# A two-layer hybrid decoder step: the second layer's heads with no arithmetic on GpSimd, rotary steps and weight splits one at a time, latents normalised once, and an opening in halves

## The chip, the core and the metric

The kernel runs on one core of one Trainium2 chip. The metric is the time of one execution on the device in microseconds. The engines are called by their names in the profile: PE is TensorE (matrix products and transposes), PEld its weight loads, DVE is VectorE, ACT is ScalarE, POOL is GpSimd, SP is SyncE, which here only issues transfers.

## What is computed

One inference step of a decoder with two layers of width 1024, for a prompt of 512 tokens and eight sample streams of four tokens each. Prompt and samples use the same weights, so the kernel keeps them as 512 + 32 = 544 columns. Cut to what matters here:

```python
# layer 0 (mixer A): input projection, pooling branch, memory attention, gates, output projection
# between the layers: one shared compressed key/value side
kv = rmsnorm(x, g_kv_in) @ w_kv_down
ckv, krope = rmsnorm(kv[..., :256], g_kv_latent), rope(kv[..., 256:])       # ranks 256 and 64
# layer 1 (mixer B): latent attention with 8 heads, and 4 heads into 256 memory tokens
z = rmsnorm(x, g_norm[1]) @ w_in_b
c_q, gate_t, q_m, gate_m = split(z)                                         # c_q has rank 384
q = (rmsnorm(c_q, g_q) @ w_q_up).reshape(T, 8, 128 + 64)
q_rope = rope(q[..., 128:])
q_lat = einsum('thd,chd->thc', q[..., :128], w_k_up)
s = (q_lat @ ckv.T + q_rope @ krope.T) * 192 ** -0.5                         # causal mask
o_lat = softmax(s) @ ckv
tok = einsum('thc,chd->thd', o_lat, w_v_up)
mixed = concatenate([tok * silu(gate_t), mem_o * silu(gate_m)])
x = x + mixed @ w_out[1]                                                    # then the last rmsnorm
```

The samples also attend, in layer 1, to 4096 earlier tokens each, which lie in a paged cache of 128 tokens a page (latent and rotary part, 32 pages to a stream).

## The kernel before

The stream is held with its features on the partitions. Products of 32-bit floats are made as three products of a reduced format: `split` (its lines are 89 and 90) writes a rounded copy, the high part, on ScalarE, and then the remainder, the low part, on VectorE or, where it is given that engine, on GpSimd. `mm3` (lines 94, 95 and 96) multiplies high by high, high by low, and low by high.

Up to the middle of the second layer a scheduler sets the order of the instructions on each engine. `normed` (lines 180 to 199) makes the two parts of the stream times the gain, one group of 128 features at a time, with `Copy` on ScalarE (line 198) and the remainder on VectorE (line 199). In the opening, `first_w` splits the first two units of weights between these steps, half a unit at a time; a unit (128x1024) is loaded whole, and line 177 (180 for later groups) is the square for the norm.

From the second layer's late gates to the output, the order on TensorE and on the queue of SP is written by hand: generators hand out pieces of TensorE's work, and `weave` picks at each step, among those that may go on, the one that is furthest behind its share. It keeps an estimated time `now` and estimated queues `act` and `dve` for ScalarE and VectorE, and a piece is taken only when its inputs are ready by these estimates. The generators are

- `round_scores` and `round_values`: sixteen rounds in which 16 pages of one stream are read from the cache (tiles `a` and `b`), some keys turned and copied (`kt`, line 1073 on ScalarE and 1076 on VectorE), the scores made (`ac`, line 1109), their maximum taken on VectorE (line 1118), the exponentials on ScalarE (`rt`, line 1120), turned again (TensorE line 135, copied by line 1135) and multiplied by the values (line 1143);
- `gates_late`: the last four gates of the layer, with `gate_part` (lines 264 and 265 are its sigmoid and its product);
- `head_inputs`: for each of the four pairs of heads a rotary projection (`q_proj`, whose eviction at line 1292 multiplies by the scale and the norm), the rotary step (`rope_T`: copies that swap halves at lines 767 and 768, products and the sum, here on GpSimd; then `qr`, a high part at line 1310 and a remainder on GpSimd at line 1311), and for each head its query and its key, and for each pair its values (`values`); every weight comes through `ahead`, is split with its remainder on GpSimd, and its successor's transfer is issued by GpSimd at that point (line 1212 for `qw`, line 1222 for `wu`);
- `scores` and `heads`: a head's own 512 by 512 scores (`hs`), softmax and output;
- `out_all`, `out_rows` and the rest: the output projection in twelve slabs of weights of 256 by 512, prepared by `prepare` three ahead, with the inputs split by `mix_b`.

Order and estimates are fixed when the kernel is built; on the chip each engine goes through its own list and waits where an input is late. The gates that the heads read late are stored to memory by GpSimd (`gd`, line 1202) and read back (`gl`, line 1375).

## Time and profile before

| what | value |
|---|---|
| time, three runs | 831.43, 831.79 and 832.11 us, median 831.79 |
| the profiled execution's own time | 830.44 us |
| its span, first to last instruction | 828.7 us |
| mean granted clock of TensorE | 0.985 of full speed |
| PE busy | 782.6 us, 94% of the span |
| DVE, ACT, POOL busy | 491.5, 316.1 and 236.2 us |
| moved by DMA | 169.54 MB, mean 205 GB/s |

The span in 40 equal slices (20.7 us each) gives the stages; each digit is the busy share in tenths, PEclk the granted clock in tenths of full speed:

```profile
PE   6999999999999999889999997899979989899995
...
DVE  6757667698834435866666644457675666742413
ACT  7453334432433325434333222345443445431212
POOL 0035221111234313303323244424232241024421
PEclk9999999999999999999999999899999999999997
```

The first layer takes the slices up to about 16, the shared key/value side and the second layer's projections run to about 480 us, the heads from about 490 to 722 us, and the output projection from there to the end. The chain of work that ended last, followed back from the last instruction, divides over the engines so:

```profile
PE 80%; DVE 9%; DMA 3%; ACT 3%; issue 2%; POOL 1%; SPq 1%; POOLq 0%; DVEq 0%; ACTq 0%
```

In the rows of the profile that list single instructions, the columns are start (us from the span's start), length, engine, line of the source, operation, output and inputs, shapes, how many of them, and in square brackets the idle time of the engine just before with what ended it. In rows that list groups, busy time and mean length in ns stand behind the bar.

### The profile page before, as it was taken

The page shows a single profiled execution, that of the slowest core. Times are in us where ns is not written, and L with a number is a line of the kernel's source. Part 1 is how long each engine was busy: PE and PEld are TensorE (multiplying, and loading weights), DVE is VectorE, ACT ScalarE, POOL GpSimd, SP SyncE. Part 2 cuts the span into 40 slices and gives each one's busy share as a digit, 9 for nine tenths or more (in the row PEclk, how much of TensorE's full clock was granted, in tenths as well). Part 3 has the DMA queues.
Part 4 walks back from the last instruction along what each step waited for, and adds up shares of the span by engine and source line. Part 5 has one row for each costly group of instructions (what it writes and reads, how often), then busy time and mean ns, then how long its engine had stood idle before and what let it go on. Part 6 is the DMA issues. An engine that isn't in the chain of part 4 may idle for free.

```text
span 828.7 us, 17366 instructions
## 1 busy us (share of the span) xinstructions
PE 782.6 (94%) x6814; PEld 666.3 (80%) x6814; DVE 491.5 (59%) x945; ACT 316.1 (38%) x631; POOL 236.2 (28%) x216
## 2 busy tenths in 40 slices
PE   6999999999999999889999997899979989899995
PEld 6989998999999989768998885567757766577774
DVE  6757667698834435866666644457675666742413
ACT  7453334432433325434333222345443445431212
POOL 0035221111234313303323244424232241024421
PEclk9999999999999999999999999899999999999997
DMA  8356247521232327436525799889868869893935
GB/s 308 95 181 226 77 178 256 159 80 63 78 96 79 100 97 230 142 127 204 204 77 206 241 352 368 297 275 334 294 228 300 302 219 353 299 343 106 327 111 177
DMA packets 82964, 169.54 MB, mean 205 GB/s; under 512 B 9409, under 2 KB 26434, under 8 KB 82626
## 3 DMA queue, kind: packets, MB, share of 16 engines
q1 hardware_dynamic: 76642, 148.04, 53.0%
q0 software_dynamic: 6240, 20.39, 6.7%
q8 instruction: 54, 0.88, 0.4%
q14 instruction: 28, 0.23, 0.1%
HBM read 157.19 MB, written 11.21 MB: 203 GB/s over the span
## 4 chain that ended last, share of the span: by engine, by line
PE 80%; DVE 9%; DMA 3%; ACT 3%; issue 2%; POOL 1%; SPq 1%; POOLq 0%; DVEq 0%; ACTq 0%
PE pa L94 16%; PE pa L96 16%; PE pa L95 15%; PE tr L135 4%; PE ac L1143 4%; PE ac L1109 3%; PE hs L94 2%; PE hs L96 2%; PE hs L95 2%; PE ac L1099 2%; PE ac L393 1%; DMA wr<-in_w_mem_v 1%; PE hs L135 1%; PE po L94 1%; DMA b<-in_cache_P 1%
## 5 line engine op out<-in xcount | busy, mean ns | idle before, releaser
L94 PE MATMUL pa<-h,wh 128*128 128x272 f32 x832 | 239.3, 290 | 0.0
L96 PE MATMUL pa<-h,wl 128*128 128x272 f32 x832 | 236.4, 289 | 1.2 <-POOL wl L90 1.2
L95 PE MATMUL pa<-h,wh 128*128 128x272 f32 x640 | 183.8, 288 | 0.0
L90 POOL TENSOR_TENSOR wl<-wr,wh 128x1024 fp32r<-128x1024 f32 (+1 forms) x54 | 121.9, 2257 | 188.9 <-ACT wh L89 185.8
L94 PEld LDWEIGHTS pa<-h,wh 128*128 128x128 f32 x832 | 156.4, 188 | 5.3 <-issue 4.3
L96 PEld LDWEIGHTS pa<-h,wl 128*128 128x128 f32 x832 | 155.0, 188 | 2.7 <-POOL wl L90 1.8
L89 ACT CAST wh<-wr 128x1024 fp32r<-128x1024 f32 (+1 forms) x87 | 87.7, 1008 | 180.5 <-PE pa L95 68.5
L95 PEld LDWEIGHTS pa<-h,wh 128*128 128x128 f32 x640 | 120.3, 188 | 0.9
L95 PE MATMUL pa<-g,wh 128*128 128x272 f32 x192 | 54.6, 289 | 0.7 <-DVE g L90 0.7
L90 DVE TENSOR_TENSOR wl<-wr,wh 128x1024 fp32r<-128x1024 f32 x33 | 40.4, 1223 | 16.4 <-ACT wh L89 16.3
L265 DVE SCALAR_TENSOR_TENSOR g<-t,g 128x272 f32<-128x272 f32 x40 | 36.0, 908 | 7.1 <-ACT t L264 7.1
L1143 PE MATMUL ac<-a,rt 128*32 128x256 f32 x384 | 37.1, 423 | 3.2 <-DVE rt L1135 3.2
L264 ACT ACTIVATE t<-g 128x272 f32<-128x272 f32 x40 | 16.6, 427 | 57.5 <-DVE g L251 57.5
L95 PEld LDWEIGHTS pa<-g,wh 128*128 128x128 f32 x192 | 36.2, 189 | 1.0 <-DVE g L90 1.0
L1143 PE MATMUL ac<-b,rt 128*32 128x256 f32 x128 | 36.8, 423 | 0.0
L1109 PE MATMUL ac<-kt,c 128*32 128x256 f32 x128 | 32.9, 380 | 2.6 <-ACT kt L1073 1.7
L1109 PE MATMUL ac<-a,c 128*32 128x256 f32 x384 | 33.4, 380 | 0.0
L1143 PEld LDWEIGHTS ac<-a,rt 128*32 128x32 f32 x384 | 14.3, 118 | 18.7 <-issue 6.9
L251 DVE SCALAR_TENSOR_TENSOR g<-pa,r 128x272 f32<-128x272 f32 x38 | 16.3, 437 | 21.6 <-PE pa L96 21.5
L1357 ACT ACTIVATE e<-hs,s 128x128 f32<-128x128 f32 (+3 forms) x32 | 16.9, 529 | 29.5 <-DVE s L1355 29.5
L95 PE MATMUL pa<-wl,mh 128*128 128x512 f32 x64 | 25.2, 402 | 1.0 <-DVE wl L90 1.0
L199 DVE SCALAR_TENSOR_TENSOR h<-x,c,h 128x544 fp32r<-128x544 f32 x24 | 19.6, 828 | 9.2 <-ACT h L198 9.1
(438 smaller groups left out, 1840.2 us busy)
## 6 DMA issues: line engine op xcount, KB each, us to landing
a<-in_cache_P SPq DMA_DIRECT2D x192, 288.0 KB, 5.5
wr<-in_w_in_a SPq DMA_DIRECT2D x24, 512.0 KB, 3.9
b<-in_cache_P SPq DMA_DIRECT2D x64, 160.0 KB, 5.8
wr<-in_w_in_b SPq DMA_DIRECT2D x19, 512.0 KB, 3.6
cs<-in_mem_kT SPq DMA_DIRECT2D x16, 512.0 KB, 5.2
wr<-in_w_out_a SPq DMA_DIRECT2D x16, 384.0 KB, 3.1
ws<-in_w_out_b SPq DMA_DIRECT2D x12, 512.0 KB, 6.1
wr<-in_w_out_b SPq DMA_DIRECT2D x9, 512.0 KB, 7.2
```

The costliest lines, as they stand in the source:

```text
L89: nc.scalar.copy(h, src)
L90: (eng or nc.vector).tensor_tensor(out=l, in0=src, in1=fr(h), op=ALU.subtract)
L94: nc.tensor.matmul(out, lhsT=wh, rhs=xh, start=start, stop=False)
L95: nc.tensor.matmul(out, lhsT=wh, rhs=xl, start=False, stop=False)
L96: nc.tensor.matmul(out, lhsT=wl, rhs=xh, start=False, stop=stop)
L135: nc.tensor.transpose(out, in_, ident[:k, :k])
L199: nc.vector.scalar_tensor_tensor(out=l, in0=xT[k], scalar=gain(base, k), in1=fr(h), op0=ALU.mult, op1=ALU.subtract)
L264: nc.scalar.activation(th[:, :HALF], z[:, o : o + HALF], AF.Tanh)
L265: nc.vector.scalar_tensor_tensor(out=z[:, o : o + HALF], in0=th[:, :HALF], scalar=1.0, in1=z[:, o : o + HALF], op0=ALU.add, op1=ALU.mult,)
L1109: nc.tensor.matmul(o[j * NS : (j + 1) * NS, :], lhsT=QT[:, k, b, :], rhs=nat[ih][0][:, 2 * j : 2 * j + 2, c] if j < 3 else kt[ih][:, k], s ...
L1143: nc.tensor.matmul(po[j * NS : (j + 1) * NS, :256], lhsT=pT[:, i * P + j * NS : i * P + (j + 1) * NS], rhs=nat[i // 2][j // 3][:, 2 * j % ...
L1357: nc.scalar.activation(e, ps[:, :n], AF.Exp, bias=nx, accum_out=sm)
```

## The change

Six things are edited; the numbers of most lines move with them.

1. The opening. The first two units of weights are loaded in halves, the first ahead of the second group of the stream, the second behind the fourth. `first_w` splits a quarter of both units at a time, at groups 0, 1, 3 and 5. ScalarE gets a square of one column of ones as its first activation, and TensorE ten products of a constant 128x128 tile.
2. The query latents. Gain and norm are applied once to the three groups of latents, with the scale of the scores multiplied into the norm on ScalarE. A query projection is then split straight from PSUM, and the eviction at line 1292 is gone.
3. The late gates' remainders are made on VectorE.
4. The heads. Two generators `weights_ahead`, one for the query weights and one for the pairs' weights, split one piece at a time as soon as the estimated queues of ScalarE and VectorE are nearly empty, on those two engines. A generator `ropes` does the rotary steps one at a time on the same condition: four copies on ScalarE, products, sum and remainders on VectorE. `head_inputs` may start at once, 7 us of estimated time earlier than before.
5. The output. A generator `first_slabs` splits the inputs and the weights of the first three slabs one at a time on the same condition; `out_all` may start at once, 12 us of estimated time earlier.
6. The later slabs' remainders are made on VectorE.

The diff, cut to its core:

```diff
 for k in range(KD):
     nc.sync.dma_start(xT[k], A["x_T"][k])
-    if k < 2:
-        nc.sync.dma_start(first[k].rearrange("p (k c) -> p k c", k=KD), A["w_in_a"][20 + k])
+    if k in (0, 3):
+        c = slice(k and 4, k + 4 + (k > 0))
+        for i in range(2):
+            nc.sync.dma_start(
+                first[i].rearrange("p (k c) -> p k c", k=KD)[:, c, :], A["w_in_a"][20 + i][:, c, :]
+            )
+nc.scalar.activation(st(1), ones, AF.Square)
+idle = ones.broadcast_to([P, P])
+ps = ps_("tr")
+for _ in range(10):
+    nc.tensor.matmul(ps[:, :P], lhsT=idle, rhs=idle, start=True, stop=True)
...
-hx = normed(G_N, {0: (0, 0), 1: (1, 0), 3: (0, 1), 4: (1, 1)}, first_w)
+hx = normed(G_N, {0: (0, 2), 1: (2, 4), 3: (4, 6), 5: (6, 8)}, first_w)
...
 for k in range(3):
-    nc.vector.tensor_scalar_mul(cq[k], cq[k], gain(G_Q, k))
-    nc.vector.tensor_copy(cqs[:, k, :], cq[k][:, SEQ:])
-    cqx.append(split(pc("c", F32R), pc("c", F32R), cq[k][:, :SEQ]))
+    nc.vector.tensor_scalar_mul(cqs[:, k, :], cq[k][:, SEQ:], gain(G_Q, k))
+nc.scalar.activation(rq[:, :SEQ], rq[:, :SEQ], AF.Copy, scale=MLA_SCALE)
+for k in range(3):
+    z = cq[k][:, :SEQ]
+    nc.vector.scalar_tensor_tensor(out=z, in0=z, scalar=gain(G_Q, k), in1=rq[:, :SEQ], op0=ALU.mult, op1=ALU.mult)
+    cqx.append(split(pc("c", F32R), pc("c", F32R), z))
...
-                late_s.append(split_w(late_w.pop(0), KD, P, nc.gpsimd))
+                dve(act(now[0], 1.12), 1.3)
+                late_s.append(split_w(late_w.pop(0), KD, P))
...
+    def weights_ahead(raw, load, total, tags, n_cols, at):
+        for n in range(total):
+            yield lambda: n < 2 or at[n - 2][0] is None
+            yield lambda: act.free <= now[0] + 0.2 and dve.free <= now[0] + 0.4
+            t = split(pat(tags[0], F32R), pat(tags[1], F32R), raw.pop(n))
+            done = dve(act(now[0], width(n_cols, 0.6)), width(n_cols, 0.69))
+            at[n] = [t, done]
+            if n + 2 < total:
+                raw[n + 2] = load(n + 2)
+            yield 0.0, 5.0 if n else 0.0
...
-        nc.vector.scalar_tensor_tensor(
-            out=out, in0=ps, scalar=MLA_SCALE, in1=rq[:, :SEQ], op0=ALU.mult, op1=ALU.mult
-        )
-        banks["pa"].until[bank] = dve(now[0] + 1.0, 0.69)
+        q_at[n][0] = None
+        banks["pa"].until[bank] = take(ps)
...
+    def ropes():
+        for j in range(4):
+            yield lambda: j in rope_x and rope_x[j][1] <= now[0]
+            x = rope_x[j][0]
+            sw, y = pt("t", n=SEQ), pt("t", n=SEQ)
+            at = 0.0
+            def free(queue):
+                return lambda: at <= now[0] and queue.free <= now[0] + 0.2
+            for r in range(0, P, 32):
+                yield free(act)
+                o = r ^ 32
+                nc.scalar.copy(sw[o : o + 32, :], x[r : r + 32, :])
+                at = act(now[0], 0.62)
+            for a, b in ((y, x), (sw, sw)):
+                yield free(dve)
+                nc.vector.tensor_tensor(out=a, in0=b, in1=tab[a is sw], op=ALU.mult)
+                at = dve(now[0], 0.69)
...
-    hi = Thread(head_inputs(), 24 / total, 94 / total, 48.0, now[0] + 7.0)
+    first = [
+        Thread(weights_ahead(raw_q, load_q, 12, ("qh", "ql"), 384, q_at), -2.0, 0.0, 1.0, now[0]),
+        Thread(weights_ahead(raw_pair, load_pair, 8, ("wuh", "wul"), 512, pair_at), -1.5, 0.0, 1.0, now[0]),
+        Thread(ropes(), -1.0, 0.0, 1.0, now[0]),
+    ]
+    hi = Thread(head_inputs(), 24 / total, 94 / total, 48.0, now[0])
...
-    wh, wl = split(fin("wh", F32R), fin("wl", F32R), t, nc.vector if (fh, s) < (0, 3) else nc.gpsimd)
+    wh, wl = split(fin("wh", F32R), fin("wl", F32R), t)
...
+    def first_slabs():
+        raw = [fin("wr") for s in range(3)]
+        for s, t in enumerate(raw):
+            slab(t, *slabs.pop(0), nc.gpsimd)
+        at = now[0] + 4.0
+        for s in range(3):
+            yield lambda: gt[order[s][1]] is not None
+            mix = [(k, load_mix(k)) for k in order[s]]
+            for k, t in mix:
+                yield lambda: act.free <= now[0] + 0.2 and dve.free <= now[0] + 0.4
+                mix_b(k, t)
+                dve(act(now[0], 0.57), 0.69)
+            yield lambda: at + 2.0 * s <= now[0] and act.free <= now[0] + 0.2 and dve.free <= now[0] + 0.4
+            prepared.append(prepare(0, s, raw[s]))
+            prepared_at.append(dve(act(now[0], 1.04), 1.2))
...
-    out = Thread(out_all(), 112 / total, 66 / total, 66.0, now[0] + 12.0)
-    weave([rv, rs, ha, os_, out], [ha, os_])
+    fs = Thread(first_slabs(), -1.0, 0.0, 1.0, now[0])
+    out = Thread(out_all(), 112 / total, 66 / total, 66.0, now[0])
+    weave([fs, rv, rs, ha, os_, out], [fs, ha, os_])
```

How the instructions stand on three engines, at the places that the change moves most. First ScalarE at the start of the program, before and then after; `x` is the stream, `h` a high part of the stream or of the weights `wr`, `c` holds constants and gains, `t` takes squares.

```order
1 L198 ACT_TABLE_LOAD
2 L198 ACTIVATE h_120<-x_86,c_84 128x544
3 L177 ACTIVATE t_259<-x_86 128x544
4 L89 CAST h_114<-wr_94 128x512 x2
5 L198 ACTIVATE h_126<-x_87,c_84 128x544
```

```order
1 L152 ACT_TABLE_LOAD
2 L152 ACTIVATE s_108<-c_80 128x1
3 L208 ACTIVATE h_137<-x_86,c_84 128x544
4 L187 ACTIVATE t_282<-x_86 128x544
5 L89 CAST h_129<-wr_94 128x256 x2
6 L89 CAST h_131<-wr_95 128x256 x2
7 L208 ACTIVATE h_145<-x_87,c_84 128x544
```

The table load now belongs to the square of a constant, which needs no transfer; a quarter of each unit is rounded ahead of the second group, where half of the first unit was.

Second, TensorE where the heads begin, at the end of a round's scores (`ac`); `tr` are transposes of the exponentials `rt`, `pa` query projections, `qh` and `ql` parts of query weights, `c` the latents. Before:

```order
3409 L1109 MATMUL ac_6135<-kt_6167,c_4074 32x256
3410 L1109 MATMUL ac_6135<-a_5725,c_4074 32x256 x3
...
3413 L135 MATMUL tr_6200<-c_79,rt_6198 128x128 x4
3414 L135 MATMUL tr_6207<-c_79,b_6059 128x128 x4
3415 L1143 MATMUL ac_6214<-a_5698,rt_6205 32x256 x3
```

and after:

```order
3412 L1123 MATMUL ac_6159<-kt_6191,c_4098 32x256
3413 L1123 MATMUL ac_6159<-a_5749,c_4098 32x256 x3
3414 L94 MATMUL pa_6242<-c_4077,qh_6203 128x512
...
3423 L94 MATMUL pa_6260<-c_4077,qh_6209 128x512
...
3428 L96 MATMUL pa_6260<-c_4082,ql_6210 128x512
3429 L135 MATMUL tr_6275<-c_79,rt_6240 128x128 x4
```

Fifteen products of a query projection (nine of `pa_6242` and six of `pa_6260`) now stand between the scores and the transposes of their exponentials.

Third, GpSimd at the same place, where `gd` are gates in memory, `qw` and `wu` query and pair weights. Before:

```order
118 L1375 DMA gl_8460<-gd 128x512
119 L90 TENSOR_TENSOR ql_6314<-qw_5636,qh_6313 128x384
120 L90 TENSOR_TENSOR wul_6346<-wu_5640,wuh_6345 128x512
...
122 L90 TENSOR_TENSOR wul_6413<-wu_5642,wuh_6412 128x512
123 L1212 DMA qw_6317<-in_w_q 128x384
124 L1202 DMA gd<-t_5999 128x512
```

and after, GpSimd and then VectorE:

```order
114 L1434 DMA gl_8502<-gd 128x512
115 L1227 DMA qw_6207<-in_w_q 128x384
...
118 L1237 DMA wu_6253<-in_w_v_up 128x2x256
119 L1217 DMA gd<-t_6023 128x512
```

```order
540 L261 SCALAR_TENSOR_TENSOR t_6023<-po_6060,r_3458 128x272
541 L90 TENSOR_TENSOR ql_6204<-qw_5660,qh_6203 128x384
542 L90 TENSOR_TENSOR ql_6210<-qw_5662,qh_6209 128x384
543 L90 TENSOR_TENSOR wul_6232<-wu_5664,wuh_6231 128x512
544 L90 TENSOR_TENSOR wul_6250<-wu_5666,wuh_6249 128x512
545 L275 SCALAR_TENSOR_TENSOR t_6023<-t_6183,t_6023 128x272
```

GpSimd only issues transfers there, and the four remainders stand on VectorE between the two halves of the last gate.

More of the change, by code (lines that the diff above doesn't have):

```diff
@@ L1245, in pat, with pair_weights @@
         return next(p for p in (hq, heads_val, heads_in) if tag in p.tags)(tag, dt, n)
[L1247 to L1257 removed]
+    def weights_ahead(raw, load, total, tags, n_cols, at):
[8 more added lines that the diff above has]
+            yield 0.0, 5.0 if n else 0.0
+    q_at, pair_at = {}, {}
+    def pair_weights(n):
+        return [t.rearrange("p (k c) -> p k c", k=2) for t in pair_at[n][0]]
     def values(j):
[L1260 removed]
+        n = 2 * j + 1
+        yield lambda: n in pair_at and pair_at[n][1] <= now[0]
+        wh, wl = pair_weights(n)
         valued_by[j] = []
@@ L1277, in values, with q_proj @@
             valued_by[j].append((vh, vl, banks["pa"].until[bank]))
+            if s0:
+                pair_at[n][0] = None
             yield 0.7, 0.0
-    def q_proj(out):
-        for t in ahead(raw_q, load_q, 12):
-            qh, ql = split(pat("qh", F32R), pat("ql", F32R), t, nc.gpsimd)
-        act(now[0], 0.47)
-        yield lambda: banks["pa"].open()
+    def q_proj(n, take):
+        yield lambda: n in q_at and q_at[n][1] <= now[0] and banks["pa"].open()
+        qh, ql = q_at[n][0]
         bank = banks["pa"].take()
@@ L1336, in head_inputs @@
                 yield from values(j)
+    def ropes():
[15 more added lines that the diff above has]
+                at = dve(now[0], 0.69)
+            yield free(dve)
+            nc.vector.tensor_tensor(out=y, in0=y, in1=sw, op=ALU.add)
+            at = dve(now[0], 0.69)
+            rope_of[j] = []
+            for half in range(2):
+                a, b = 64 * half, 64 * (1 - half)
+                s = pat("qr", F32R)
+                yield free(act)
+                nc.scalar.copy(s[a : a + 64, :], y[a : a + 64, :])
+                at = act(now[0], 0.62)
+                yield free(dve)
+                nc.vector.tensor_tensor(
+                    out=s[b : b + 64, :], in0=y[a : a + 64, :], in1=fr(s)[a : a + 64, :], op=ALU.subtract
+                )
+                at = dve(now[0], 0.69)
+                rope_of[j].append((s, at + 0.3))
     def scores():
```

93 lines of the change are left out of this document (43 added, 50 removed).

## The prediction

> **What bounds the kernel now.** I read the busy shares first, then a table of the span in stretches, then who TensorE waits for, then the instructions around its longest waits. The shares (busy us, share of the span, instructions):
>
> ```profile
> PE 782.6 (94%) x6814; PEld 666.3 (80%) x6814; DVE 491.5 (59%) x945; ACT 316.1 (38%) x631; POOL 236.2 (28%) x216
> ```
>
> TensorE sets the time wherever it does not wait, and the change leaves its products alone but for ten constant ones at the start. So what can be won is the 46 us in which it has nothing and the stretches at half clock. Where they lie (columns: stretch, its length, busy us of PE, PEld, DVE, ACT, POOL with instructions, granted clock, DMA share, GB/s):
>
> ```profile
> 7.10:11.40 4.30, 4.30 (x18) 4.14 (x19) 4.30 (x7) 4.30 (x8) 0.00 (x0) 1.00 1.02 397
> 11.40:21.00 9.60, 9.60 (x79) 9.60 (x78) 9.60 (x14) 8.64 (x15) 0.00 (x0) 1.00 0.85 327
> 29.00:331.00 302.00, 299.99 (x2405) 285.38 (x2404) 192.12 (x325) 115.55 (x207) 80.11 (x65) 1.00 0.42 133
> 331.00:376.00 45.00, 40.04 (x266) 31.54 (x265) 33.27 (x70) 18.29 (x29) 8.57 (x6) 1.00 0.44 139
> ...
> 509.00:524.00 15.00, 8.83 (x103) 5.08 (x106) 6.28 (x12) 4.24 (x10) 7.96 (x10) 0.77 0.94 340
> 524.00:540.00 16.00, 13.62 (x128) 9.86 (x123) 9.59 (x11) 6.78 (x13) 9.96 (x10) 1.00 0.77 278
> 540.00:612.00 72.00, 71.43 (x756) 52.47 (x749) 46.34 (x117) 32.57 (x83) 22.11 (x24) 1.00 0.91 314
> 612.00:626.00 14.00, 9.35 (x89) 5.07 (x88) 9.79 (x17) 5.86 (x14) 8.25 (x7) 0.88 0.37 117
> 626.00:665.00 39.00, 38.71 (x390) 28.89 (x388) 24.80 (x60) 16.09 (x42) 7.98 (x10) 1.00 0.92 320
> 665.00:674.00 9.00, 6.76 (x66) 3.91 (x65) 6.09 (x8) 4.78 (x11) 7.46 (x7) 0.81 0.19 68
> 674.00:700.00 26.00, 25.90 (x257) 18.91 (x255) 16.24 (x41) 13.17 (x32) 2.98 (x7) 1.00 1.00 358
> 700.00:722.00 22.00, 18.70 (x218) 12.40 (x222) 14.42 (x41) 9.41 (x21) 2.53 (x4) 0.92 0.87 291
> ```
>
> The first layer is full (299.99 of 302). The heads of the second layer are full too (71.43 of 72, 38.71 of 39, 25.90 of 26) except in five places: 509 to 540, 612 to 626, 665 to 674 and 700 to 722, which lack 6.17 + 2.38 + 4.65 + 2.24 + 3.30 = 18.7 us. In four of them the clock falls as well. A mean of 0.77 over 15 us is 6.9 us at half speed, 0.88 over 14 is 3.4, 0.81 over 9 is 3.4, 0.92 over 22 is 3.5: 17.2 us, in which at most half, 8.6 us, is lost. Together 27.3 us hang on these places, and in the first four POOL is busier than anywhere between them (7.96 of 15 and 7.46 of 9, against 7.98 of 39). The first of them, instruction by instruction (start, length, what, and idle time before with its cause); TensorE:
>
> ```profile
> 511.96 0.40 PE L1109 MATMUL ac<-kt,c 128*32 128x256 f32 x1 [1.57 <-ACT kt L1073]
> 516.85 1.12 PE L135 MATMUL tr<-c,rt 128*128 128x128 f32 x4 [3.82 <-ACT rt L1120]
> 518.75 1.11 PE L135 MATMUL tr<-c,b 128*128 128x128 f32 x4 [0.78 <-DVE rt L1135]
> ```
>
> and ScalarE, VectorE and GpSimd ahead of it:
>
> ```profile
> 509.46 0.51 ACT L89 CAST qh<-qw 128x384 fp32r<-128x384 f32 x1 [3.34 <-PE po L96]
> ...
> 511.33 0.57 ACT L1073 COPY kt<-tr 128x512 f32<-128x512 f32 x1
> ...
> 512.27 2.90 DVE L265 SCALAR_TENSOR_TENSOR t<-t,t 128x272 f32<-128x272 f32 x1 [2.42 <-ACT t L264]
> ...
> 515.30 0.68 DVE L1118 TENSOR_REDUCE s<-ac 128x1 f32<-128x512 f32 x1
> ...
> 511.43 1.28 POOL L90 TENSOR_TENSOR wul<-wu,wuh 128x512 fp32r<-128x512 f32 x1
> 512.66 0.99 POOL L90 TENSOR_TENSOR ql<-qw,qh 128x384 fp32r<-128x384 f32 x1
> 513.62 1.25 POOL L90 TENSOR_TENSOR wul<-wu,wuh 128x512 fp32r<-128x512 f32 x1
> ```
>
> The VectorE step at 512.27 takes 2.90 us over 272 columns and ends when GpSimd's last split ends (514.87); the softmax maximum behind it (L1118) starts at 515.30, and TensorE stands 3.82 us for the exponentials. The same kind of step at 472.10 below takes 2.39 us. The third place is alike:
>
> ```profile
> 613.99 2.08 DVE L768 COPY t<-t 32x512 f32<-32x512 f32 x2
> 617.86 1.72 DVE L1164 TENSOR_TENSOR s<-c,s 128x1 f32<-128x1 f32 x1
> 618.27 1.27 POOL L771 TENSOR_TENSOR t<-t,t 128x512 f32<-128x512 f32 x1
> 620.92 0.42 PE L1143 MATMUL ac<-a,rt 128*32 128x256 f32 x3 [2.92 <-DVE rt L1135]
> ```
>
> A subtraction of one column takes 1.72 us until the rotary step on GpSimd ends at 619.54. The Trainium skill ("SBUF — State Buffer", section "SBUF: two separate sides") says that VectorE and GpSimd share a pair of SBUF ports under an exclusive lock, held for a whole instruction, for which a VectorE step with two SBUF inputs must wait. The trace agrees: 2.90 us against the three splits.
>
> **The change part by part.** The sum is made against the profiled execution's 830.44 us (span 828.7); the median of the three runs, 831.79, lies 1.35 above it.
>
> *The opening.*
>
> ```profile
> 3.95 1.28 ACT L198 ACT_TABLE_LOAD   x1 [3.95 <-DMA x<-in_x_T]
> 5.24 0.75 ACT L198 ACTIVATE h<-x,c 128x544 fp32r<-128x544 f32 x1
> 6.44 1.12 ACT L89 CAST h<-wr 128x512 fp32r<-128x512 f32 x2
> 7.10 0.59 PE L94 MATMUL pa<-h,h 128*128 128x272 f32 x1 [7.10 <-ACT h L89]
> ```
>
> The table load now stands ahead of the wait for the first input, so the three steps behind it move up by 1.28, and the cast of a quarter (256 columns for 512, some 0.3 us of the 0.56) ends sooner: first product at about 5.5. That holds if the half weight tile, now split into two transfers, has landed; gain 1.3 to 1.6. The ten constant products are there to have TensorE busy before. 18 products in 4.30 us are 0.239 each, 79 in 9.60 are 0.122: the cold start costs 18 x 0.117 = 2.1. The transposes at 518.75 in a half-speed stretch come 0.2 apart, so ten constant products are some 2 us, over by about 3.1, with 2.4 us of nothing behind. I take 1.1 of the 2.1. Opening: -2.5, between -1.3 and -3.7. VectorE must keep up afterwards (9.60 of 9.60 busy in 11.4 to 21), which is why I do not take more. The rule of the Trainium skill ("TensorE: Matmul & The Clock Gate", Part 1) is that a busy free-running window of about 3.4 us releases the clock. Ten products fill less than one, and by the rule alone the opening would give the 1.4 without the 1.1; no run here shows which.
>
> *Latents normalised once.* Three products by the gain become three with rq in them, ScalarE scales rq once, and twelve evictions (first row below) go, since the query products are then split straight from PSUM.
>
> ```profile
> L1292 DVE SCALAR_TENSOR_TENSOR t<-pa,r 128x512 f32<-128x512 f32 x12 | 8.3, 688 | 6.2 <-PE pa L96 6.1
> L768 DVE COPY t<-t 32x512 f32<-32x512 f32 x8 | 8.8, 1106 | 0.3
> L767 ACT COPY t<-t 32x512 f32<-32x512 f32 x8 | 4.9, 617 | 0.9 <-DVE t L1292 0.8
> L90 POOL TENSOR_TENSOR ql<-qw,qh 128x384 fp32r<-128x384 f32 x12 | 12.2, 1019 | 27.0 <-ACT qh L89 18.8 <-ACT s L1165 8.2
> L1311 POOL TENSOR_TENSOR qr<-t,qr 64x512 fp32r<-64x512 f32 x8 | 10.2, 1279 | 6.9 <-ACT qr L1310 6.6
> L90 POOL TENSOR_TENSOR wul<-wu,wuh 128x512 fp32r<-128x512 f32 x8 | 10.2, 1274 | 25.9 <-ACT wuh L89 25.7
> 345.86 0.85 PE L836 MATMUL ac<-wq,c 128*32 128x384 f32 x8 [1.26 <-DVE c L811]
> ```
>
> In the stretch 331 to 376 the one wait that these steps end is the last row's 1.26; the step it waits for (L811) is gone, another of the kind may take its place. Between -1.3 and +1.3, taken at 0.
>
> *Late gates.* Four splits of weights go from GpSimd to VectorE.
>
> ```profile
> 472.10 2.39 DVE L265 SCALAR_TENSOR_TENSOR g<-t,g 128x272 f32<-128x272 f32 x1 [0.89 <-ACT t L264]
> 474.95 0.33 PE L135 MATMUL tr<-c,e 128*128 128x128 f32 x1 [0.81 <-DVE e L441]
> ```
>
> Without the 2 us that the first row waits, the second's 0.81 goes: -0.8 (0 if VectorE's own 128x1024 split stands in the same place).
>
> *The heads.* All of GpSimd's arithmetic goes to VectorE: 12 splits of 384 columns, 8 of 512, 8 rotary remainders and 12 rotary steps, at 0.69 for 512 columns (L1292's size) 6.2 + 5.5 + 5.5 + 8.3 = 25.5 us. It loses 8.3 (L1292) and the 8.8 of L768's swaps: +8.4, less what it now spends waiting on GpSimd. ScalarE gets the swaps (8 more of 0.62) and four copies of the rotary part: +7.3. In the full stretch 540 to 612 they are busy 46.34 and 32.57 of 72, so both have room on the mean; what counts is the order. With the lock's waits gone, 6.17 + 2.38 + 4.65 + 2.24 shrink. At the first place the order now has 15 products of 512 columns ahead of the transposes that wait for the exponentials, 3.5 us at 0.23 each, so the 3.82 is covered twice: by an earlier maximum and by other work. The cluster at 700 has little GpSimd work (2.53 of 22); there a burst of splits for the output is spread out by the new thread.
>
> What comes back: the 1.57 before 511.96 stays, as four casts still stand ahead of that copy. Four swaps in a row on ScalarE are 2.5 us for 1.2 before, up to 1.3 late at each of four rotary heads: 5.2. Half of the last cluster stays, 1.7 + 0.9 of clock, and one other half-speed window, 1.7. That is 11.1 of 27.3, which leaves -16.2. Ends: -27 when nothing comes back, -4 when the waits come back on ScalarE and VectorE at the same places.
>
> *Output slabs.* Nine splits of 1024 columns move to VectorE, which is idle for most of 722 to 808 with TensorE full; hidden, 0, and up to +1 if they delay the sample rows.
>
> Sum: -2.5 + 0 - 0.8 - 16.2 + 0 = -19.5, so 810.9 for a profiled execution like this one, and about 812 on the scale of the median; I put 811.
>
> **The rivals.**
> 1. *The pages bind.* DMA runs at 358 GB/s with a share of 1.00 in 674 to 700, and at 314 in 540 to 612; it rests in the waits (117 and 68 GB/s), which is when it catches up. With 16 us less over 509 to 722 the mean rises by some 8%. If the pages then come late at half of the sixteen rounds, by 1 us each, 8 us return: 819. For it: 1.00. Against: 0.91 and 0.92 in the other full stretches.
> 2. *The waits move.* ScalarE's swap bursts and VectorE's longer queue hold the evictions that TensorE waits for as often as GpSimd did: opening, gates and -4, 824. For it: the waits already name ACT kt and ACT rt. Against: between the rotary steps nothing waits.
> 3. *Slower: late weights at the head of VectorE's queue.* A split now blocks everything behind it until its load, issued by GpSimd behind stores that wait for VectorE, has landed. 16 of the 20 splits have loads issued during the heads. It decides from 16 x 1.4 = 22 us, where all gains are gone; at 1.6 each, 836. Against: a load has two other splits between its issue and its use. The Trainium skill ("SBUF — State Buffer", section "SBUF: two separate sides") names a cause by which such loads could come later, that VectorE's copies keep GpSimd from writing descriptors; no run here shows it.
> 4. *The opening does nothing*: constant products over too early, weights not there: -0.5 for -2.5, 813, inside the range.
>
> **How the numbers follow.** Forecast with rival 4, 804 to 818: 0.58. More (all 27 us, or below 804): 0.08. Pages: 0.13. Waits move: 0.11. Slower: 0.07. No change, by two of these together: 0.03. The range 803 to 824 leaves out most of the first extreme and the slower cases. A measurement of this kernel tells about 0.2% (1.7 us) from no change. Faster 0.90, same 0.03, slower 0.07.
>
> **What would show it.** Right: no GpSimd arithmetic between 480 and the end but the last scalings; L265's form at 0.44 throughout the heads; idle time of TensorE over the heads below 9 us and at most two half-speed windows; first product near 5.5. Wrong: TensorE waiting on ACT at the swaps (rival 2), on DMA a or b (rival 1), VectorE's splits idle on DMA qw or wu (rival 3), products still 0.24 apart until 11 (rival 4).

## The result, and the profile after

The changed kernel took 816.52 to 819.06 us in four runs, median 818.47, beside 831.61 for the kernel before on the same chip: a ratio of 0.9844 with an interval of 0.9817 to 0.9871, some 13 us faster. The forecast was 811, with a range of 803 to 824. Run again later, the same kernel gave 0.9896 (0.9874 to 0.9918), 822.7 against 830.8; where those 4 us lie is shown below. One execution of the run e3 below took 1258 us at a granted clock of 0.57 and is left out of its figures. The profiled execution of the changed kernel took 819.06 us (span 817.2), 11.4 less than that of the kernel before.

The profile's first line, then the table of stretches (columns as in the prediction, some of its stretches; the changed kernel's work stands a few us off from the old one's at the same time):

```profile
PE 782.2 (96%) x6834; PEld 668.8 (82%) x6834; DVE 495.6 (61%) x982; ACT 324.0 (40%) x649; POOL 156.1 (19%) x163
```

```profile
331.00:376.00 45.00, 39.02 (x257) 32.44 (x256) 31.50 (x62) 17.59 (x27) 8.14 (x6) 0.92 0.41 130
...
509.00:524.00 15.00, 13.33 (x142) 8.87 (x138) 10.07 (x22) 9.35 (x19) 4.15 (x7) 1.00 1.02 368
524.00:540.00 16.00, 15.71 (x178) 11.67 (x171) 9.20 (x18) 7.07 (x16) 3.07 (x5) 1.00 0.98 353
540.00:612.00 72.00, 68.62 (x699) 50.64 (x700) 50.63 (x132) 38.24 (x94) 5.27 (x9) 1.00 0.87 299
612.00:626.00 14.00, 14.00 (x161) 10.41 (x161) 7.11 (x18) 4.64 (x12) 0.55 (x1) 1.00 0.97 332
```

TensorE is full or nearly so at 509 to 540 and 612 to 626, where it lacked 13.2 us and now lacks 2.0, and the clock no longer falls there. The stretch 540 to 612, full before, now lacks 3.4. Not all of that is new: the transposes of the eighth round waited 1.69 us in the kernel before, at the start of the hole at 613 to 621, and since that round now comes 5 us earlier, what is left of the hole stands in the other stretch. The two rows, before and after:

```profile
615.62 0.66 PE L135 MATMUL tr<-c,rt 128*128 128x128 f32 x4 [1.69 <-ACT rt L1120]
```

```profile
610.38 0.66 PE L135 MATMUL tr<-c,rt 128*128 128x128 f32 x4 [1.36 <-ACT rt L1134]
```

And the clock now falls in 331 to 376, where it did not: 0.92 over 45 us is 7.2 us at half speed (mean 0.66 in the ten us behind 355).

Where the time went is read most sharply from the starts of the same product in both traces, since the products themselves are the same. The difference is that of the changed kernel against the one before, and the last column the step in it:

| the product | before | after | difference | step |
|---|---|---|---|---|
| first product of the stream | 7.10 | 5.77 | -1.33 | |
| first memory product | 35.30 | 35.44 | +0.14 | opening +0.14 |
| last statistics ahead of the second layer | 304.92 | 305.05 | +0.13 | 0 |
| first key transposes of the second memory branch | 386.65 | 388.84 | +2.19 | latents +2.06 |
| values of the first round of pages | 503.72 | 505.15 | +1.44 | late gates and around -0.76 |
| last page transposes | 750.58 | 737.27 | -13.31 | heads -14.75 |
| last product | 817.97 | 806.55 | -11.42 | output +1.89 |

### The profile page after: what moved, and what is told of

It is laid out like the page before. It is cut to its first block, busy times and chain, and to the rows that moved or that the text cites. A ratio compares the mean times of both kernels' runs of the same rounds, so it can differ in the third digit from the quotient of the medians.

```text
span 817.2 us, 17409 instructions
## 1 busy us (share of the span) xinstructions
PE 782.2 (96%) x6834; PEld 668.8 (82%) x6834; DVE 495.6 (61%) x982; ACT 324.0 (40%) x649; POOL 156.1 (19%) x163
## 4 chain that ended last, share of the span: by engine, by line
PE 78%; DVE 7%; ACT 6%; DMA 4%; issue 2%; POOL 1%; SPq 1%; POOLq 0%; DVEq 0%; ACTq 0%
PE pa L94 15%; PE pa L95 15%; PE pa L96 15%; PE tr L135 4%; PE ac L1157 3%; PE ac L1123 3%; PE hs L94 2%; PE hs L95 2%; PE hs L96 2%; PE ac L1113 2%; PE ac L403 1%; PE hs L135 1%; POOL wl L90 1%; ACT t L1373 1%; ACT wh L89 1%
## 5 line engine op out<-in xcount | busy, mean ns | idle before, releaser
L90 POOL TENSOR_TENSOR wl<-wr,wh 128x1024 fp32r<-128x1024 f32 (+1 forms) x41 | 90.6, 2210 | 134.5 <-ACT wh L89 134.4
L90 DVE TENSOR_TENSOR wl<-wr,wh 128x1024 fp32r<-128x1024 f32 x46 | 56.1, 1223 | 39.2 <-ACT wh L89 39.0
L275 DVE SCALAR_TENSOR_TENSOR g<-t,g 128x272 f32<-128x272 f32 x40 | 32.7, 829 | 5.6 <-ACT t L274 5.6
L1157 PE MATMUL ac<-a,rt 128*32 128x256 f32 x384 | 31.4, 383 | 0.2
L1157 PE MATMUL ac<-b,rt 128*32 128x256 f32 x128 | 31.2, 383 | 0.0
L1157 PEld LDWEIGHTS ac<-a,rt 128*32 128x32 f32 x384 | 14.0, 109 | 14.1 <-issue 2.8
L90 DVE TENSOR_TENSOR p<-hs,p 128x512 fp32r<-128x512 f32 (+3 forms) x32 | 15.0, 487 | 16.1 <-ACT p L89 15.8
```

The lines of the kernel that those rows point to most:

```text
L90: (eng or nc.vector).tensor_tensor(out=l, in0=src, in1=fr(h), op=ALU.subtract)
L275: nc.vector.scalar_tensor_tensor(out=z[:, o : o + HALF], in0=th[:, :HALF], scalar=1.0, in1=z[:, o : o + HALF], op0=ALU.add, op1=ALU.mult,)
L1157: nc.tensor.matmul(po[j * NS : (j + 1) * NS, :256], lhsT=pT[:, i * P + j * NS : i * P + (j + 1) * NS], rhs=nat[i // 2][j // 3][:, 2 * j % ...
```

## The experiments

Besides the times (ratios against the kernel before on the same chip, with intervals), the table gives the same steps from each profile. "Old" and "new" name which opening, latents, heads and slabs a kernel has; "pool" is GpSimd.

| run | what differs | ratio (interval) | opening | latents | heads | output |
|---|---|---|---|---|---|---|
| changed, first | | 0.9844 (0.9817 to 0.9871) | +0.1 | +2.1 | -14.7 | +1.9 |
| e15 | changed, again | 0.9896 (0.9874 to 0.9918) | -0.8 | +7.5 | -15.0 | +1.9 |
| e3 | old opening | 0.9908 (0.9876 to 0.9941) | +0.3 | +4.2 | -14.7 | +1.9 |
| e7 | old loads and splits | 0.9892 (0.9864 to 0.9919) | +2.1 | +2.8 | -15.5 | +1.9 |
| e9 | as e7, no constant products | 0.9868 (0.9836 to 0.9900) | +0.8 | +1.5 | -13.0 | +1.9 |
| e14 | kernel before, new opening | 1.0007 (0.9995 to 1.0019) | -0.3 | -0.1 | -0.1 | 0.0 |
| e6 | kernel before, new latents | 1.0032 (1.0021 to 1.0043) | +1.0 | +1.5 | +0.4 | 0.0 |
| e1 | sample queries made first | 0.9875 (0.9860 to 0.9890) | -1.0 | +4.7 | -12.3 | +1.7 |
| e12 | norm ahead of sample queries | 0.9954 (0.9937 to 0.9971) | -0.1 | +8.9 | -14.4 | +1.9 |
| e13 | e12, late slabs on pool | 0.9920 (0.9901 to 0.9939) | -0.5 | +8.5 | -12.4 | 0.0 |
| e2 | changed, late slabs on pool | 0.9848 (0.9815 to 0.9882) | -0.3 | +3.2 | -15.1 | 0.0 |
| e4 | heads' arithmetic on pool | 0.9894 (0.9879 to 0.9910) | -0.6 | +2.0 | -11.3 | +1.9 |
| e5 | kernel before, heads' arithmetic on VectorE | 0.9878 (0.9860 to 0.9896) | +0.2 | -0.4 | -8.0 | 0.0 |

The four steps leave out two stretches, so they do not add up to the ratio (between 35 and 305 us the kernels lose 0 to 1.3 us, e7 most; between 389 and 504 seven stand 0.8 to 1.3 us better than the kernel before, e3 1.9 worse, where pages came late). They come from one profile each. How far these scatter is seen from the kernels that share a step: the nine with the new heads as they are have -12.3 to -15.5, mean -14.1.

### The opening: e3, e7, e9 and e14

e3 undoes the opening in the changed kernel, e7 keeps the square and the constant products but loads and splits as before, e9 drops the constant products as well, and e14 is the kernel before with only the new opening.

```diff
 e3, e7 and e9:
-        if k in (0, 3): ... halves of both units
+        if k < 2:
+            nc.sync.dma_start(first[k]..., A["w_in_a"][20 + k])
-hx = normed(G_N, {0: (0, 2), 1: (2, 4), 3: (4, 6), 5: (6, 8)}, first_w)
+hx = normed(G_N, {0: (0, 0), 1: (1, 0), 3: (0, 1), 4: (1, 1)}, first_w)
 e3 and e9:
-for _ in range(10):
-    nc.tensor.matmul(ps[:, :P], lhsT=idle, rhs=idle, start=True, stop=True)
 e3:
-nc.scalar.activation(st(1), ones, AF.Square)
```

> The changed kernel with its opening undone: whole units loaded as before, halves split as before, no square and no constant products. Theory A (VectorE's full queue from 8 to 22 us sets the end of the opening, so the constant products and the early table load buy nothing): the time stays at 818.5 within 1, and by 35 us the products stand within 0.3 us of where they stand in the changed kernel. Theory B (the opening was worth the forecast 2.5 and the lag seen at 35 us is noise or made elsewhere): 820.5 to 821.

> The changed kernel with the loads and the splits of the weights as before, but with the square (early table load) and the ten constant products. Theory A: VectorE starts its first step at 4.9 instead of 6.0 and does not wait for a second transfer, so 1.0 to 1.4 us less than the changed kernel, 817.2, with products 1.0 to 1.4 earlier at 35 us. Theory B (the clock is what the opening lacks): 3.3 less than with the opening undone. If quarters and halves matter for the start: no gain, 818.5.

> As the run before, without the ten constant products: loads and splits as before, early table load kept. Theory A: the same as with them within 0.5 us, 817.2, because VectorE and not the clock of TensorE paces the opening. Theory B: 2 us slower than with them.

> The kernel before with only the opening of the changed kernel. Theory A (VectorE's queue sets the end of the opening): first product at 5.8, but products within 0.5 us of the kernel before at 35 us, and the time the same within 1 us, 831.6. Theory B (the opening is worth the forecast 2.5): 829.

The opening's single rows of the changed kernel, TensorE, then ScalarE and VectorE, and its stretch from 11.4 to 21:

```profile
0.90 4.63 PE L156 MATMUL tr<-c 128*128 128x128 f32 x20 [0.90 <-POOL c L132]
5.77 0.57 PE L94 MATMUL pa<-h,h 128*128 128x272 f32 x2 [0.23 <-ACT h L89]
7.88 0.39 PE L94 MATMUL pa<-h,h 128*128 128x272 f32 x1 [1.04 <-ACT h L89]
11.91 0.39 PE L95 MATMUL pa<-h,h 128*128 128x272 f32 x1 [0.39 <-DVE h L209]
```

```profile
7.43 0.71 ACT L89 CAST h<-wr 128x256 fp32r<-128x256 f32 x2 [1.40 <-DMA wr<-in_w_in_a]
7.86 0.76 DVE L90 TENSOR_TENSOR l<-wr,h 128x256 fp32r<-128x256 f32 x2 [1.35 <-ACT h L89]
```

```profile
11.40:21.00 9.60, 8.75 (x66) 8.20 (x65) 9.60 (x17) 9.47 (x18) 0.00 (x0) 1.00 0.85 329
```

Both things that the opening is for happened: the first product starts 1.33 us earlier, and the ten constant products (20 rows, since each is recorded in two, 0.21 apart) last 4.63 us, after which the clock is full for the real products, 0.13 us apart where they do not wait. The rule that the prediction took from the Trainium skill ("TensorE: Matmul & The Clock Gate", Part 1) fits the eight kernels with the new opening, whose clock is full by 4.1 to 5.9 us: their constant products can fill a window of activity, only because they took 4.0 to 4.6 us and not the 2 I had put. In e7 the same ten products did not do it (below). But TensorE runs into its inputs. ScalarE waits 1.40 us for the next piece of weights, VectorE 1.35 behind it, and then VectorE works from 8.9 to 22 without a pause (9.60 of 9.60 us in the last row, as before), with eight splits of 0.38 where there were four of 0.65. TensorE, full in that stretch before, has 8.75 of it, and its waits of 0.2 to 0.4 end on VectorE.

e14 settles what that is worth: 1.0007, no change, as theory A said; its interval leaves room for a gain of 0.4 us. In its profile the first product came at 6.75, though, and not at the 5.8 expected. Over all profiles, the eight kernels with the new opening stand at -0.45 us at the first memory product on the mean (-1.0 to +0.1), and the three others with the old one, e3, e6 and e5, at +0.5 (+0.2 to +1.0): a gain of about 1 us, if it is one. Part of it would be the clock. In the five kernels without constant products the clock is full from 11.3 (the kernel before), 11.7 (e5), 12.1 (e3), 13.3 (e9) and 13.5 us (e6), and in the same order their first memory product stands at 0, +0.2, +0.3, +0.8 and +1.0. So the profile of the kernel before, which the prediction read, has the earliest clock of the five, and the constant products had least to win against it.

In e7 theory A failed. It expected products 1.0 to 1.4 us ahead of the changed kernel, and from 15 to 24 us they stand 1.3 ahead of it (1.0 ahead of the kernel before), although the clock did not come early. Its constant products are the same and end 0.64 us ahead of the first real one, but the real ones stay 0.23 us apart until 10.2 us, the sign that I had named for rival 4:

```profile
6.17 0.60 PE L94 MATMUL pa<-h,h 128*128 128x272 f32 x1 [0.64 <-ACT h L89]
6.56 0.43 PE L95 MATMUL pa<-h,h 128*128 128x272 f32 x1
```

The changes of the clock in one trace are whole multiples of 3.41 us apart; in e7 they stand at 10.2, 27.3 and 30.7, so one such step ended at 6.8, and the 0.64 us without work lie in it. That this kept the clock down is argued, not shown. Then TensorE waits 1.42 us for the norm, and the clock falls behind that wait:

```profile
26.05 0.82 PE L135 MATMUL tr<-c,s 128*128 128x128 f32 x5 [1.42 <-POOL s L165]
```

```profile
21.00:29.00 8.00, 6.58 (x46) 5.99 (x45) 3.66 (x13) 0.74 (x2) 1.20 (x1) 0.89 0.22 72
29.00:35.00 6.00, 6.00 (x44) 6.00 (x43) 4.44 (x10) 2.46 (x6) 0.00 (x0) 0.86 0.02 3
```

So the lead turned into a wait, and the wait into 2.1 us lost at 35 us. The wait comes with the order: in e7 two products stand between the last of the statistics and the transposes that wait for the norm, in the kernel before fourteen, in the changed kernel thirty. e9, without the constant products, has fourteen and no such wait; it was expected at 817.2 like e7 and took 820.24 beside e7's 822.31, with intervals that overlap. The time of e3 alone would have spoken for theory B (823.71 us, not 818.5). Its profile puts none of that at the opening (+0.3): 2.6 us are a wait for a transfer at 347, next.

### The latents: e6, e1, e12, and the changed kernel again

```diff
 e6, on the kernel before (the query projections' eviction becomes a plain copy):
-    nc.vector.tensor_scalar_mul(cq[k], cq[k], gain(G_Q, k)) ... as in the change
-        nc.vector.scalar_tensor_tensor(out=out, in0=ps, scalar=MLA_SCALE, in1=rq[:, :SEQ], ...)
+        nc.vector.tensor_copy(out, ps)
 e1, on the changed kernel, the latents' block behind sample_q():
+        nc.vector.scalar_tensor_tensor(out=gq, in0=q[:, :3], scalar=0.0, in1=gT[:, G_Q : G_Q + 3], op0=ALU.mult, op1=ALU.add)
-        ... out=z, in0=z, scalar=gain(G_Q, k), in1=rq[:, :SEQ] ...
+        ... out=z, in0=z, scalar=gq[:, k : k + 1], in1=rq[:, :SEQ] ...
 e12, on the changed kernel:
-        nc.vector.tensor_scalar_mul(cqs[:, k, :], cq[k][:, SEQ:], gain(G_Q, k))
+        nc.vector.scalar_tensor_tensor(out=cqs[:, k, :], in0=cq[k][:, SEQ:], scalar=gain(G_Q, k), in1=rq[:, SEQ:], ...)
-        rq4, its transpose, rcol
```

> The kernel before with only the latents' gain and norm applied once; the query projections' evictions become plain copies, as many as before. Theory A (the change of the latents loses time between 331 and 390 us, since the scheduler now puts the sample queries' transposes on TensorE ahead of the memory products, and they wait for VectorE): products at 390 us stand 2 to 3 us later than in the kernel before, TensorE waits 3 us or more at the transposes of a near 356, and the time is 833.5. Theory B (the loss came from the shifted opening): no loss there, 831.

> The changed kernel with the three products of the latents made dependent on the sample queries (their gains come from a sum with zero times the sample queries), so that VectorE makes the sample queries first. Theory A: the wait of 3.95 us at 359.5 shrinks to 1 to 1.5, products at 390 us stand about 2 us earlier, 816 to 816.5. Rival (another step of the sample queries ends the wait, or the reordered products wait elsewhere): 818.5.

> The changed kernel again, on the chip of the three that follow, as their base: 818 to 820. Its products stand within 0.5 us of the kernel before's at 35 us, 1.5 to 3 behind at 390, and TensorE waits some 3.9 us at the transposes of a near 356 and 1.6 near 761, since these come with the order and not with a run.

> The changed kernel with the norm multiplied into the samples' latents too, ahead of their query products, and the separate column of norms left out. Theory A (the loss between 331 and 390 is an order in which TensorE stands at the sample queries' transposes while the memory products are ready behind them): eight memory products now stand ahead of the transposes, the 3.95 us of wait shrink to under 1.5, products at 390 us stand 2 us earlier than in the changed kernel, and the time is 2 us less. Rival (a longer chain from norm to sample queries is waited for at the next place): no gain.

Who TensorE waits for between 325 and 400 us (total, times, longest) in the kernel before, in e6 and in e12:

```profile
PE pa L94 <- ACT wh L89: 1.7, 2, 1.4
PE ac L836 <- DVE c L811: 1.3, 1, 1.3
```

```profile
PE tr L135 <- DVE a L855: 4.0, 1, 4.0
PE ac L839 <- DVE c L810: 1.3, 1, 1.3
```

```profile
PE ac L852 <- DVE g L261: 4.8, 1, 4.8
PE tr L194 <- DVE t L191: 2.3, 1, 2.3
```

The new latents alone bring the wait of 4.0 us into the old kernel, cost 1.5 us at 389, and 1.0032 in time. What they changed is an order. VectorE and then TensorE in the changed kernel:

```profile
354.77 2.08 DVE L825 SCALAR_TENSOR_TENSOR c<-c,c,r 128x512 f32<-128x512 f32 x3 [0.34 <-ACT r L822]
...
357.02 1.23 DVE L90 TENSOR_TENSOR wl<-wr,wh 128x1024 fp32r<-128x1024 f32 x1
...
358.77 0.61 DVE L866 TENSOR_SCALAR a<-ac,s 128x384 f32<-128x384 f32 x1
...
359.52 0.66 PE L135 MATMUL tr<-c,a 128*128 128x128 f32 x2 [3.95 <-DVE a L866]
```

The samples' latents were copied after the gain had gone over all 544 columns; now they are made at once, so the scheduler places the samples' query products and transposes earlier. In the kernel before, twelve memory products stand ahead of the transposes of `a`; in the kernels with the new latents, but for e12 and e13, none does. The transposes then wait for VectorE, which first has the new products over 512 columns and a weight split in its queue, and the clock falls behind the wait.

The changed kernel, run again, has the 3.8 us at `a` as expected, and a second wait: at 389 us it stands 6.75 behind, where 1.5 to 3 were expected, and it took 822.7 for 818 to 820. How long the three transfers of the sample queries' weights (`wq`) take from issue to landing, in the kernel before, in the first profile of the changed kernel, and in the second:

```profile
DMA to landing us min/median/max: 5.5/5.6/5.7
```

```profile
DMA to landing us min/median/max: 7.4/8.2/9.1
```

```profile
DMA to landing us min/median/max: 8.6/9.6/10.7
```

and the issue of the third by SP in the kernel before, and in the second profile of the changed one with the product that reads it:

```profile
343.08 0.57 SPq L834 DMA_DIRECT2D wq<-in_w_q  x1
```

```profile
336.85 0.57 SPq L848 DMA_DIRECT2D wq<-in_w_q  x1
...
347.68 0.85 PE L850 MATMUL ac<-wq,c 128*32 128x384 f32 x8 [3.79 <-DMA wq<-in_w_q]
```

Before, it was issued at 343.08 and read at 350.84. Now it is issued 5 to 6 us earlier, among weights for the layer's projection and the stores of the latents, takes two to five us longer, and is read 3 to 4 us sooner. Whether it is late differs from profile to profile: not in the first, by 3.79 us in the second, by 2.6 in e3, 3.2 in e1. What decides it stays open. Most of the difference between the two results of the changed kernel lies here: products at 389 us are 393.40 against 388.84.

The two attempts to mend it failed, and the rivals that I had named took the place. In e1 the wait of 3.95 became 1.0, but the next step of the sample queries is waited for 3.1 and the transfer 3.2. In e12, with 22 memory products ahead of the transposes, nothing waits at `a`, but the sample queries wait for the norm and VectorE's gates: 4.8 and 2.3, and the stage is 8.9 us late. What order of that stage would cost nothing stays open.

### The heads: e4 and e5

e4 keeps the new order and puts the arithmetic back on GpSimd; e5 keeps the old order and moves the arithmetic to VectorE.

```diff
 e4:
-            t = split(pat(tags[0], F32R), pat(tags[1], F32R), raw.pop(n))
+            t = split(pat(tags[0], F32R), pat(tags[1], F32R), raw.pop(n), nc.gpsimd)
 and in ropes() nc.vector becomes nc.gpsimd for the two products, the sum and the remainders
 e5:
-            qh, ql = split(pat("qh", F32R), pat("ql", F32R), t, nc.gpsimd)
+            qh, ql = split(pat("qh", F32R), pat("ql", F32R), t)
 likewise the pairs' weights, rope_T(...) and the rotary remainders
```

> The changed kernel with the order of its planner kept, but the remainders of the heads' weights and the rotary products, sums and remainders on GpSimd again. Theory A (VectorE's steps that wait behind GpSimd's steps made the holes): VectorE's steps in 490 to 720 are some 10 us longer in sum than now, TensorE's waits there go from 10 to about 18 us with the clock falling behind them, and the time is 826 to 829. Theory B (the order did it: steps one at a time, an earlier start of the heads): at most 3 us are lost, 821.

> The kernel before with its old order, and only the heads' arithmetic moved from GpSimd to VectorE. Theory A: VectorE's long steps in the heads go, the first hole at 512 to 517 shrinks, and 6 to 10 us are won, 822 to 825. Theory B: in the old order the splits and rotary steps come in bursts on the one queue that TensorE waits for, so nothing is won or it is slower, 831 to 836.

VectorE in the changed kernel, in e5 and then in e4, at the place of the first hole:

```profile
513.66 0.44 DVE L275 SCALAR_TENSOR_TENSOR t<-t,t 128x272 f32<-128x272 f32 x1
```

```profile
512.50 0.44 DVE L265 SCALAR_TENSOR_TENSOR t<-t,t 128x272 f32<-128x272 f32 x1
```

```profile
512.51 2.76 DVE L275 SCALAR_TENSOR_TENSOR t<-t,t 128x272 f32<-128x272 f32 x1 [2.37 <-ACT t L274]
```

and who TensorE waits for between 480 and 740 us, the longest rows of the kernel before, of e5, and of e4, and the first of the changed kernel:

```profile
PE tr L135 <- ACT rt L1120: 9.0, 5, 3.8
PE ac L1143 <- DVE rt L1135: 3.2, 2, 2.9
```

```profile
PE tr L135 <- ACT rt L1120: 6.4, 5, 2.0
PE ac L1109 <- ACT kt L1073: 1.7, 2, 1.6
```

```profile
PE hs L135 <- DVE e L1418: 2.5, 3, 1.1
PE ac L1123 <- ACT kt L1087: 2.5, 3, 1.5
```

```profile
PE ac L1123 <- ACT kt L1087: 2.5, 3, 1.5
PE tr L135 <- ACT rt L1134: 1.9, 3, 1.4
```

Moving the arithmetic alone won 8.0 us, the rest of the change without it 11.3, both together 14.1 on the mean (12.3 to 15.5). The rest is the order, and with it the query evictions that are gone and the swaps that are all on ScalarE; what of the 11.3 is the order alone was not run. Each covers most of what the other does: with the arithmetic off GpSimd the late maximum comes earlier, with the new order TensorE has products to do until it comes. In e4 VectorE's steps are stretched again, the one at 512.5 to 2.76 us for 0.44, and the scalings of the softmax as below, changed kernel and e4, some 14 us in sum over 500 to 725; yet that costs some 3 us only (1 to 4, by the spread), and TensorE's waits between 480 and 740 sum to 14.1 us for 10.1.

```profile
L1418 DVE TENSOR_SCALAR e<-e,s 128x128 f32<-128x128 f32 x8 | 2.2, 279 | 0.0
```

```profile
L1418 DVE TENSOR_SCALAR e<-e,s 128x128 f32<-128x128 f32 x8 | 5.6, 697 | 0.1
```

Theory A was right on the mechanism and wrong on its share: it gave 826 to 829 for e4, measured were 822.5, nearer to the 821 of the order, and no slower than the changed kernel's second result; of the 18 us of waits that it named, 14.1 came. For e5 it held (822.5 in 822 to 825), and theory B with its bursts did not: four splits in a row cost VectorE 2.5 us ahead of the step at 512.50, but they are over when it comes.

### The slabs: e2 and e13

```diff
-        wh, wl = split(fin("wh", F32R), fin("wl", F32R), t)
+        wh, wl = split(fin("wh", F32R), fin("wl", F32R), t, nc.vector if (fh, s) < (0, 3) else nc.gpsimd)
```

> The changed kernel with the remainders of the later slabs (the fourth on) on GpSimd again. Theory A (on VectorE the split of the second half's first slabs stands ahead of the evictions of the sums, which holds the banks, and TensorE waits 1.64 us at 762 for them): 1.9 less, 816.6, and no wait of TensorE at that place. Rival (the wait is made by the order of TensorE or by the loads): no change, 818.5. Rival (GpSimd's splits hold VectorE's evictions): slower, 819 to 820.

> As the run before, and the remainders of the fourth and later slabs on GpSimd. If both losses are what they were read to be they add up: 2.0 + 1.9 less than the changed kernel, so 4 us, about 815. If GpSimd's splits cost what they save: 2 us less.

e13 is e12 with this edit.

The changed kernel where the second half of the output begins, VectorE and TensorE:

```profile
760.59 1.22 DVE L90 TENSOR_TENSOR wl<-wr,wh 128x1024 fp32r<-128x1024 f32 x1 [0.39 <-ACT wh L89]
761.73 1.28 DVE L1577 TENSOR_TENSOR x<-hs,x 128x512 f32<-128x512 f32 x2
...
762.47 0.50 PE L94 MATMUL hs<-wh,c 128*128 128x512 f32 x1 [1.64 <-DVE x L1577]
```

The split of 1.22 us stands ahead of the evictions of the first half's sums, and TensorE has no bank until they are done. With these splits on GpSimd the wait is gone in e2 and in e13, and the output's step is 0.0 in both where it is +1.9 (e1: +1.7) in the other kernels with VectorE's splits. In time e2 (817.88) and the changed kernel (818.47) can't be told apart, since the runs of one kernel spread over 2 to 6 us; e13 stands at 0.9920 where e12 has 0.9954. e13 did not come out at the 815 expected, as its latents are those of e12.

## Why the prediction was right, and which terms were off

The sum was -19.5, which is 812.3 on the scale of the median, where I put 811. The profiled execution moved by -11.4; the direction, the place and the main term were right, and 818.47 lies in the range, 7.5 above the forecast. The 8.1 us too much are 2.6 of the opening, 2.1 of the latents, 1.5 of the heads and 1.9 of the slabs.

- **Heads, -16.2, measured -14.7 (-14.1 on the mean of nine profiles).** The holes closed as described: the 3.82 is gone, the 1.57 stays (1.52 before 513.35), L275 takes 0.44, and of four stretches at half clock, 17.1 us in sum, one of 3.4 is left. Waits of TensorE from 480 to 740 sum to 10.1 us for 20.5; the sign that I named, under 9, was missed by one. Four swaps on ScalarE do take 2.51 us, but none of TensorE's waits ends on them, so the 5.2 that I had put back for them did not come. Other waits stand in their place: for `kt` from ScalarE and VectorE, 0.82 and 0.72 us in 540 to 612, and for the output's weights, 1.30 and 0.76 at 706 to 708; the 1.36 for `rt` is what is left of the hole at 613 to 621. So the place and the mechanism were right, and that the size came so near is in part luck.
- **The reason for the heads was half right.** The prediction put the hole down to VectorE's wait for GpSimd and gave the order as a second cover. By e4 and e5 the order, with the evictions and swaps that changed beside it, is the larger of the two, 11.3 against 8.0.
- **Opening, -2.5, measured +0.1 in the profile, no change in e14.** The step that failed is that an earlier first product and a full clock move the end of the stage. I had quoted the row that speaks against it (VectorE 9.60 of 9.60) and used it only to cap the term. In the changed kernel it was the bound: what the earlier start gave went into the waits for the next piece of weights (1.40 and 1.35). The constant products, put at 2 us, took 4.63. Rival 4 named this outcome with other causes, of which the late weights were one.
- **Latents, 0 within 1.3, measured +2.1, and +7.5 where the transfer is late.** The step that failed is "the one wait that these steps end": I looked for what the removed instructions release and not for what the scheduler would now place earlier. This is the largest miss, and outside of its own bounds.
- **Late gates, -0.8, measured -0.76** over 389 to 504, in part by luck: 0.4 of the 0.81 is still waited for, and e5, e6 and e14, whose late gates are as before, stand at -0.2 to -0.5 over the same stretch.
- **Slabs, 0 to +1, measured +1.9.** I had TensorE full as a cover, and a delay of the sample rows as the risk; what the splits delay are the evictions at the change of halves, and by more than I allowed.
- **The rivals.** Pages did not bind: waits for them between 480 and 740 sum to 0.8 us, as before. No wait for `qw` or `wu` ends an idle time of TensorE, so late weights at VectorE's head did not come. The waits moved only in the small.

## What to carry to other kernels

Where two engines block each other, price separately the removal of the block and an order that has other work ready while it lasts: here the first alone, and the rest of the change without it, each gave more than half. In a stage whose second engine is busy without a pause, an earlier start of the first engine was worth nothing here, and less than nothing in e7, where the order had a hole in which the clock fell. And where a scheduler sets the order, an edit that makes one small operand ready earlier is a move of everything behind it, transfers included: read the order, not only the instructions taken out. By the steps above, a kernel with the old latents, the new heads and the old slabs would stand some 15 us below the one before, if the heads do not need the evictions gone; it was not run.

## What the runs showed of the chip that I had not expected

A product of a constant 128x128 tile in 32-bit floats is recorded in two rows 0.21 us apart at the start of the program, so ten lasted 4.63 us, twice my estimate; they were followed by a full clock in eight kernels and not in e7. A single wait of 1.42 us of TensorE (e7, at 26 us) was followed by a fall of the clock, 0.89 in the stretch with it and 0.86 in the next. And a transfer of 768 KB landed after 5.5 us where it was issued at 343 us in the kernel before, and after 7.4 and 10.7 us in two profiles of the changed kernel, where it was issued 5 to 6 us earlier; that the other transfers beside it are the reason is argued, not shown.
